# Two-column copies on VectorE, second keys and values ahead of the third query, a tick after every k tile of the even layer

## The chip, the cores and the metric

The kernel runs on one core of one Trainium2 chip. The metric is device time in microseconds (us) of one execution. Engines are named as the profile names them: PE is TensorE (PEld its weight loads), DVE is VectorE, ACT is ScalarE, POOL is GpSimd, SP is the queue that issues nearly all DMAs.

## The reference, cut to what matters

One inference step of a two-layer trunk over 128 context tokens and 512 latent tokens (640 columns, `T`), width 2048, all fp32. Each layer is an adaLN-modulated RMS norm, one wide input projection, two mixers side by side, a SiLU gate, an output projection and a gated residual:

```python
def modulation(cond, w, b):
    m = jax.nn.silu(cond) @ w + b
    return jnp.split(m, 3, axis=-1)          # shift, scale, gate: for layer 0 and layer 1

def even_mixer(h, w_in, sink, wg, bg, gnorm, cache):
    qa, ka, va, qb, kb, vb, rb, gp = split_cols(h @ w_in, EVEN_SPLITS)
    ya = window_sink_attention(rope_2d(qa), rope_2d(ka), va, ck, cv, sink)   # 8 query heads, 2 key-value heads
    yb, s_fin = gla_branch(qb, kb, vb, rb, wg, bg, gnorm, s0)                # 4 heads, two directions
    y = jnp.concatenate([ya, yb.astype(ya.dtype)], axis=-1) * jax.nn.silu(gp)
    return y, side
...
        x = x + gate[:, None] * (y @ w_out[l])
```

The context tokens go through the same weights with plain causal-free attention; the odd layer has neighbourhood attention and a spatial-gating MLP in the two mixers' places.

## The kernel before

**Tiling.** Activations lie feature-major: 16 tiles (`KT`) of 128 features by 2 + 640 columns. The two columns in front carry the shift vectors of the two request groups, so that one matmul chain also gives the projection of the shift. A projection makes one *chunk* of 128 output features at a time: 16 k tiles, two halves of the columns (322 and 320 wide), and three matmuls each, because a fp32 product is made of two reduced-precision parts of each operand: `acth`/`actl` of the activations, `whi`/`wlo` of the weights. That is 96 matmuls of 320 or 322 columns a chunk, called projection matmuls below. A chunk's weights come by DMA into `wraw` (later `rs`), ACT makes `whi`, and POOL (sometimes DVE) subtracts to make `wlo`.

**Evacuation.** When a half of a chunk is complete in its PSUM bank, `evac` in `lin` or `gate` multiplies it by `rstd` on DVE into an SBUF tile; for the first half it also copies the two shift columns to a small tile `bc` (L1378 in `lin`, L1408 in `gate`), which a later ACT instruction adds as a bias. Until the product and the copy are both done the bank isn't free for the next half.

**Stages.** The start (modulation of layer 0, norm, first chunks) takes the first 165 us; then the gated linear attention (GLA) of the even layer, four heads, to about 510 us; then the even attention, eight heads, to about 740 us; then the output projection and the odd layer, most of it as Strassen products of chunk pairs (`spair`), to the end.

**What sets the order.** The program is written by a planner. The class `Pace` keeps a modelled clock for each engine; `Trunk.now` is PE's. The projection matmuls are the backbone. Everything else (heads, GLA steps, splits of weights, deferred halves of evacuations) is a Python generator that is advanced by `tick()`. One tick issues due DMAs, deferred evacuations, up to three weight splits, one task step, and up to four steps of the low-priority task `ada_task`. In `units` (L890 to L909), which runs the plain chunks, a tick comes after every second k tile: that is after six projection matmuls. A step is issued when `until` says that its operands are ready within 0.05 on the modelled clock.

`need(flags)` is the one place where the backbone stops: where the next evacuation needs a buffer that a head still holds, the planner moves its clock and calls `tick` until the flag comes, and no projection matmul is issued meanwhile. The engines run their queues in order, so such a place is a run of head matmuls with nothing between them.

`ada_task` computes the modulations that are needed later (names `partg`, `parts`, `part`, in the order gate 0, scale 1, shift 1, gate 1) on DVE, as reductions of 128x512 (last table 128x256) from `adas` against a row that ACT has put in a PSUM bank. It may step while DVE's modelled clock is no more than `room` ahead of PE's; `rooms` has one value for each stage.

**The even attention** (L2442 on): chunks stand in the order k0 v0 q0 q1 q2 q3 k1 v1 g0 q4 q5 g1 q6 g2 q7, where g is a gate chunk. There are two query buffers (ring `hq`), so the evacuation of query h needs flag `eq{h-2}`: head h-2 has made its last scores. A head (`even_head`, `blocks`) is a chain of five blocks: scores on PE, maximum on DVE, exponential on ACT, normalization on DVE, transposes on PE, copies on DVE and ACT, and at the end one product with the values.

```python
                pre = (f"eq{h - 2}",) if h >= 2 else ()
                add(wE[h], 128, True, None, lazy("hq", SC, pre=pre, then=qdone))
```

## Time and profile before

| | us |
|---|---|
| median of 3 runs (2110.97 to 2112.99) | 2111.03 |
| the profiled execution | 2111.34 |
| its span, first to last instruction | 2109.6 |
| mean granted TensorE clock | 0.995 |

| engine | busy, us | share of the span |
|---|---|---|
| PE | 2054.4 | 97% |
| DVE | 1518.0 | 72% |
| POOL | 1047.1 | 50% |
| ACT | 970.3 | 46% |

PE is what the other engines serve. It was idle for 55 us of the span; a shorter time has to come out of that, out of stretches in which its clock was lowered, or out of fewer matmuls. The table by stages and the waits of PE stand in the prediction.

### The profile page before, as it was taken

How to read it: one execution, taken by the hardware profiler on the slowest of the kernel's cores; microseconds unless marked ns; L12 is line 12 of the kernel's file. 1: busy time of each engine (PE TensorE's matmuls, PEld its weight loads, DVE VectorE, ACT ScalarE, POOL GpSimd, SP SyncE). 2: the span in 40 equal slices, each digit the busy share in tenths (PEclk: the TensorE clock that was granted, in tenths of full speed). 3: DMA queues.
4: the chain of work that ended last, by engine and by line, in shares of the span. 5: the costliest groups of instructions: out<-in, count | busy, mean ns of one | idle time of the engine just before them, and what ended most of it. 6: DMA issues, size and time to landing. Idle time of an engine off the chain costs nothing. (4 is left out here: it accounts for less than half of the span.)

```text
span 2109.6 us, 38920 instructions
## 1 busy us (share of the span) xinstructions
PE 2054.4 (97%) x13990; PEld 1978.4 (94%) x13990; DVE 1518.0 (72%) x3367; ACT 970.3 (46%) x2100; POOL 1047.1 (50%) x797
## 2 busy tenths in 40 slices
PE   7999999999999999999999999999999999999996
PEld 4789999999989999999999999999999999999996
DVE  1337786777887876798766898887787777776565
ACT  3334454353343445544454444444555554454443
POOL 3433343233313223476656565656555557649783
PEclk9999999999999999999999999999999999999998
DMA  9955432335544443677658756656666565568766
GB/s 373 326 190 154 128 109 93 120 125 166 175 122 161 141 148 105 212 255 235 203 138 276 258 202 215 231 192 208 214 214 213 185 234 203 168 209 261 244 199 217
DMA packets 216306, 412.48 MB, mean 196 GB/s; under 512 B 25712, under 2 KB 89008, under 8 KB 216112
## 3 DMA queue, kind: packets, MB, share of 16 engines
q1 hardware_dynamic: 214640, 408.43, 58.9%
q8 instruction: 110, 1.80, 0.3%
q10 hardware_dynamic: 1472, 1.56, 0.2%
q14 instruction: 84, 0.69, 0.1%
HBM read 368.83 MB, written 38.45 MB: 193 GB/s over the span
## 5 line engine op out<-in xcount | busy, mean ns | idle before, releaser
L394 PE MATMUL bank<-acth,whi 128*128 128x320 f32 (+1 forms) x3144 | 963.8, 318 | 12.7 <-DVE arena L208 3.5
L394 PE MATMUL bank<-acth,wlo 128*128 128x320 f32 (+1 forms) x3144 | 939.2, 310 | 5.8 <-POOL wlo L208 5.6
L394 PE MATMUL bank<-actl,whi 128*128 128x320 f32 (+1 forms) x3144 | 937.6, 310 | 0.0
L208 POOL TENSOR_TENSOR wlo<-wraw,whi 128x512 fp32r<-128x512 f32 x351 | 483.1, 1382 | 726.6 <-ACT whi L208 652.7
L394 PEld LDWEIGHTS bank<-acth,whi 128*128 128x128 f32 x3144 | 583.1, 188 | 31.3 <-issue 9.8
L394 PEld LDWEIGHTS bank<-acth,wlo 128*128 128x128 f32 x3144 | 582.7, 188 | 8.7 <-POOL wlo L208 8.7
L394 PEld LDWEIGHTS bank<-actl,whi 128*128 128x128 f32 x3144 | 583.1, 188 | 1.5
L208 POOL TENSOR_TENSOR wlo<-rs,whi 128x512 fp32r<-128x512 f32 x285 | 401.7, 1421 | 217.8 <-ACT whi L208 193.0
L208 ACT ACTIVATE whi<-wraw 128x512 fp32r<-128x512 f32 (+1 forms) x397 | 243.0, 624 | 177.0 <-PE bank L394 105.6
L208 ACT ACTIVATE whi<-rs 128x512 fp32r<-128x512 f32 x329 | 200.4, 624 | 72.1 <-PE bank L394 46.2
L208 DVE CUSTOM_DVE_ANT_0 adas<-adas,bank,partg 128x256 bf16<-128x256 f32 (+1 forms) x320 | 178.1, 556 | 17.1 <-ACT bank L208 6.9
L394 PE MATMUL bank<-tail,whi 128*128 128x322 f32 (+1 forms) x672 | 152.1, 313 | 0.0
L394 PE MATMUL bank<-eh,whi 128*128 128x322 f32 (+1 forms) x444 | 139.2, 314 | 0.0
L394 PE MATMUL bank<-eh,wlo 128*128 128x322 f32 (+1 forms) x444 | 138.0, 311 | 0.0
L394 PE MATMUL bank<-el,whi 128*128 128x322 f32 (+1 forms) x444 | 137.7, 310 | 0.0
L208 ACT ACTIVATE bc<-bank 128x2 f32<-128x2 f32 (+1 forms) x101 | 17.2, 170 | 230.4 <-DVE arena L208 148.1
L208 ACT ACTIVATE Y<-bank 128x128 f32<-128x128 f32 (+5 forms) x134 | 52.0, 411 | 133.1 <-PE bank L394 77.8
L394 PEld LDWEIGHTS bank<-tail,whi 128*128 128x128 f32 x672 | 112.3, 189 | 0.4
L208 DVE TENSOR_TENSOR rs<-rs 128x512 f32<-128x512 f32 x83 | 89.2, 1085 | 26.7 <-POOL wlo L208 26.4
L208 DVE TENSOR_TENSOR bank<-bank,sums 128x320 f32<-128x320 f32 (+1 forms) x162 | 76.4, 492 | 40.8 <-PE bank L394 33.0
L394 PE MATMUL bank<-tail,wlo 128*128 128x322 f32 (+1 forms) x336 | 104.0, 309 | 0.0
L208 ACT ACTIVATE arena<-arena,bc 128x192 f32<-128x192 f32 (+4 forms) x167 | 82.5, 518 | 42.0 <-DVE arena L208 40.2
(215 smaller groups left out, 2901.6 us busy)
## 6 DMA issues: line engine op xcount, KB each, us to landing
tail<-far_dram SPq DMA_DIRECT2D x196, 322.0 KB, 4.2
wraw<-w_even SPq DMA_DIRECT2D x176, 256.0 KB, 3.3
adas<-ada_g SPq DMA_DIRECT2D x128, 256.0 KB, 4.3
adas<-ada SPq DMA_DIRECT2D x128, 256.0 KB, 3.6
rs<-w_odd SPq DMA_DIRECT2D x63, 512.0 KB, 5.1
Y<-ada SPq DMA_DIRECT2D x37, 512.0 KB, 6.0
wraw<-w_odd SPq DMA_DIRECT2D x37, 512.0 KB, 5.3
rs<-w_out SPq DMA_DIRECT2D x30, 512.0 KB, 5.6
```

Source lines behind the costliest of these rows:

```text
L208: return f(*args, **kw)
L394: self.nc.tensor.matmul(out, lhsT, rhs, start=start, stop=stop, **kw)
```

## The change

Four edits. The two-column copies go from ACT to DVE, in `lin` and in `gate`. The chunks of the even attention are made from a list, `ORDER`, in which k1 and v1 stand ahead of q2 and q3; v1 now names its need of `v0`, since both pass through one buffer. `units` ticks after every k tile. `rooms[0]`, which holds until the even attention opens, goes from 0.3 to 0.5.

```diff
+ORDER = "k0 v0 q0 q1 k1 v1 q2 q3 g0 q4 q5 g1 q6 g2 q7".split()
...
-    rooms, calms, lags = (0.3, 1.2, 1.5, 0.8), (4.0, 2.0), (3.0, 3.0, 2.0, 1.0, 0.4)
+    rooms, calms, lags = (0.5, 1.2, 1.5, 0.8), (4.0, 2.0), (3.0, 3.0, 2.0, 1.0, 0.4)
...
                     self.mm_k(c, j, [(p[half], half)], k0)
-                    if j % 2:
+                    if True:
                         self.tick()
...
-                nc.scalar.activation(bc[:M], pa[:M, 0:2], AF.Copy, scale=scale)
+                nc.vector.tensor_scalar(bc[:M], pa[:M, 0:2], scale, None, ALU.mult)
...
-                nc.scalar.activation(bc, pa[:, 0:2], AF.Copy)
+                nc.vector.tensor_copy(bc, pa[:, 0:2])
...
-        for kv in range(2):
...
-            add(wE[8 + kv], 128, True, None, lazy("hk", then=kdone))
-            add(wE[10 + kv], 128, True, None, lazy("av", then=vdone))
-            for h in range(4 * kv, 4 * kv + 4):
-                if kv and h != 5:
-                    i = max(h - 5, 0)
-                    gate_chunk(wE[28 + i], i, (f"ya{i}",), "gx")
...
+            add(wE[10 + kv], 128, True, None, lazy("av", pre=("v0",) if kv else (), then=vdone))
...
+            add(wE[h], 128, True, None, lazy("hq", SC, pre=(f"eq{h - 2}",) if h >= 2 else (), then=qdone))
...
+        for x in ORDER:
+            n = int(x[1])
+            if x[0] == "g":
+                gate_chunk(wE[28 + n], n, (f"ya{n}",), "gx")
+            else:
+                {"k": att_k, "v": att_v, "q": att_q}[x[0]](n)
```

The built programs, instruction by instruction: PE has the same 13,200 instructions in another order (the first 1,170 and the last 2,459 stand in the same order). ACT loses 101 two-column copies and 2 table loads, DVE gains the 101 copies. Since the planner decides by its clocks which engine makes a `wlo`, 20 of them go from DVE to POOL (POOL 632 to 652, DVE 90 to 70).

The first place is on PE, in the even attention, where the second head ends. Its scores, transposes (`ident`) and products (names with `Y` and `arena`, the heads' buffers) stand here; rows with `acth` or `actl` are projection matmuls. Before:

```order
L394 MATMUL bank_67<-acth,wlo 128x322
L394 MATMUL bank_70<-Y,arena_4504 128x128
L399 MATMUL bank_71<-ident,arena_4504 128x128 x4
L394 MATMUL bank_72<-Y,arena_4504 128x128
L394 MATMUL bank_72<-arena_4504 128x128
L394 MATMUL bank_72<-Y,arena_4504 128x128
L394 MATMUL bank_70<-arena_4504 128x128
L394 MATMUL bank_70<-Y,arena_4504 128x256
L399 MATMUL bank_71<-ident,arena_4504 128x128 x4
L399 MATMUL bank_72<-ident,arena_4504 128x128
L399 MATMUL bank_70<-ident,arena_4504 128x128 x3
L394 MATMUL bank_71<-Y,arena_4504 128x128
```

The same head's last transposes on PE in the changed program:

```order
L395 MATMUL bank_67<-acth,wlo 128x320
L400 MATMUL bank_72<-ident,arena_4540 128x128 x4
L395 MATMUL bank_67<-acth,whi 128x320
L395 MATMUL bank_67<-actl,whi 128x320
L395 MATMUL bank_67<-acth,wlo 128x320
L395 MATMUL bank_67<-acth,whi 128x320
L395 MATMUL bank_67<-actl,whi 128x320
L395 MATMUL bank_67<-acth,wlo 128x320
L395 MATMUL bank_67<-acth,whi 128x320
L395 MATMUL bank_67<-actl,whi 128x320
L395 MATMUL bank_67<-acth,wlo 128x320
```

Before, 26 head matmuls follow each other with no projection matmul among them, which is the one such run in the even attention (all others have at most 7). In the changed program no run there is longer than 7, and twelve projection matmuls stand between these transposes and the next three.

The second place is on PE in the GLA, at the end of a head: eight and six products, then twelve that need a state which DVE computes after the six. Before:

```order
L394 MATMUL bank_71<-Y,arena_1682 128x128 x8
L394 MATMUL bank_72<-Y,arena_1682 128x128 x6
L394 MATMUL bank_67<-acth,whi 128x320
L394 MATMUL bank_67<-actl,whi 128x320
L394 MATMUL bank_67<-acth,wlo 128x320
L394 MATMUL bank_67<-acth,whi 128x320
L394 MATMUL bank_67<-actl,whi 128x320
L394 MATMUL bank_67<-acth,wlo 128x320
L394 MATMUL bank_70<-Y,arena_1682 128x128 x12
```

And on PE in the changed program:

```order
L395 MATMUL bank_71<-Y,arena_1680 128x128 x8
L395 MATMUL bank_72<-Y,arena_1680 128x128 x6
L395 MATMUL bank_68<-acth,whi 128x320
L395 MATMUL bank_68<-actl,whi 128x320
L395 MATMUL bank_68<-acth,wlo 128x320
L395 MATMUL bank_70<-Y,arena_1680 128x128 x12
```

Between the six and the twelve stand three projection matmuls instead of six; it is so in all four heads.

The third place is the evacuation of q0 in the even attention. Before, the copy stands on ACT, behind three splits of weights:

```order
L208 ACTIVATE Y<-bank_71 128x128
L208 ACTIVATE whi<-wraw 128x512 x3
L208 ACTIVATE bc_4910<-bank_67 128x2
L208 ACTIVATE arena_4504<-arena_4504,bc_4910 128x128
L208 ACTIVATE arena_4504<-arena_4504,bc_4910 128x512
```

In the changed program it stands on DVE, right behind the product from the same bank (the ISA rows are the reductions of `ada_task`):

```order
L209 ISA parts_103 128x1
L209 TENSOR_TENSOR arena_4540<-bank_69,rstd 128x320
L209 TENSOR_SCALAR bc_4947<-bank_69 128x2
L209 ISA adas,parts_103<-adas,bank_73,parts_103 128x512
L209 ISA parts_103 128x1
```

Nothing but the product now stands between the bank's last matmul and its copy on the same engine. The reductions of `ada_task` also stand earlier. Counted on DVE by the number of projection matmuls ahead of them: of gate 1's 128x256 reductions, 14 stand between the 6,900th and the 7,200th before and 26 now, 18 and 29 in the next 300, and 64 and 0 between the 8,400th and the 9,300th.

## Prediction

> **What bounds the kernel now.** I read the engines' busy time first, then the table by stages, then what PE waited for, then the timeline at the largest holes.

> ```profile
> PE 2054.4 (97%) x13990; PEld 1978.4 (94%) x13990; DVE 1518.0 (72%) x3367; ACT 970.3 (46%) x2100; POOL 1047.1 (50%) x797
> ```

> PE works 97% of the span, and the change takes no matmul away. So all that can be won is idle time of PE (2109.6 - 2054.4 = 55.2 us) and time at a lowered clock. The table by stages (columns: PE, PEld, DVE, ACT, POOL busy, granted clock, DMA share, GB/s) says where these lie:

> ```profile
> 0.00:50.00 50.00, 35.96 (x280) 23.94 (x280) 7.47 (x22) 19.22 (x45) 17.07 (x20) 0.97 0.98 371
> ...
> 150.00:500.00 350.00, 346.29 (x2377) 340.87 (x2377) 254.15 (x478) 161.88 (x318) 109.68 (x79) 1.00 0.37 117
> ...
> 520.00:530.00 10.00, 8.04 (x54) 7.50 (x54) 7.94 (x23) 4.29 (x9) 2.77 (x3) 1.00 0.71 247
> 530.00:590.00 60.00, 60.00 (x406) 58.57 (x405) 48.47 (x138) 22.83 (x56) 19.26 (x15) 1.00 0.54 169
> 590.00:604.00 14.00, 9.62 (x50) 7.46 (x49) 12.67 (x46) 4.51 (x17) 0.75 (x1) 0.76 0.24 76
> 604.00:830.00 226.00, 225.85 (x1495) 217.07 (x1494) 168.31 (x492) 99.75 (x237) 62.41 (x49) 1.00 0.45 142
> 830.00:1180.00 350.00, 345.12 (x2333) 343.23 (x2332) 270.49 (x628) 174.78 (x366) 207.71 (x170) 1.00 0.69 218
> 1180.00:1400.00 220.00, 216.67 (x1472) 212.79 (x1471) 188.56 (x381) 97.84 (x215) 132.37 (x93) 1.00 0.64 215
> 1400.00:2000.00 600.00, 595.64 (x3972) 581.18 (x3972) 439.94 (x920) 298.65 (x663) 378.27 (x282) 1.00 0.64 213
> 2000.00:2109.60 109.60, 91.25 (x605) 88.86 (x603) 65.98 (x100) 42.41 (x81) 65.12 (x53) 0.95 0.63 210
> ```

> Start and end hold 14.0 and 18.4 us of the idle time, and PE's order there is untouched. The odd layer and the output projections (830 to 2000) hold 4.9 + 3.3 + 4.4 = 12.6 us, spread thin. The even layer holds 3.7 us in the GLA, 2.0 us at 520 to 530, and 4.4 us at 590 to 604, the only stretch between start and end in which the clock fell (0.76). In the rest of the attention PE is idle for 0.15 us in 286. The whole of PE's waits, largest groups (us, times, longest):

> ```profile
> PE bank L394 <- POOL wlo L208: 5.6, 8, 1.2
> PE bank L394 <- DVE arena L208: 4.9, 8, 1.3
> PE bank L394 <- ACT bc L208: 3.4, 5, 1.2
> ...
> PE bank L394 <- DVE tail L208: 3.2, 2, 1.9
> ...
> PE bank L399 <- DVE arena L208: 2.7, 2, 1.4
> PE bank L399 <- ACT es L208: 1.7, 1, 1.7
> ```

> The last two rows are the hole at 594: 2.7 + 1.7 = 4.4 us.

> **The new order of keys and values.** The timeline of that hole, PE's rows with the idle time before each in brackets:

> ```profile
> 595.65 0.63 PE L399 MATMUL bank<-ident,arena 128*128 128x128 f32 x4 [1.69 <-ACT es L208]
> ...
> 597.54 0.47 PE L399 MATMUL bank<-ident,arena 128*128 128x128 f32 x1 [1.26 <-DVE arena L208]
> ...
> 599.44 0.90 PE L399 MATMUL bank<-ident,arena 128*128 128x128 f32 x3 [1.43 <-DVE arena L208]
> ```

> These are the transposes of the second head, and they are the run of 26 head matmuls of the order before: q3 was due for evacuation, its buffer was q1's, and `need("eq1")` stopped the projections until head 1 had gone through DVE and ACT block by block. With k1 and v1 ahead, q2 and q3 come two chunks later, head 1 ends between projection matmuls, and the run is gone. What is saved is the idle time, 1.69 + 1.26 + 1.43 = **4.4 us**; the 26 matmuls themselves stay. The clock fell in the same place:

> ```profile
> 596.60:600.00 3.40, 1.03 (x4) 0.74 (x5) 3.23 (x15) 1.61 (x7) 0.00 (x0) 0.50 0.01 3
> 600.00:603.40 3.40, 3.40 (x10) 2.34 (x9) 2.60 (x11) 0.28 (x1) 0.00 (x0) 0.50 0.26 77
> ```

> For 6.8 us it was half. PE worked for 1.03 + 3.40 = 4.43 us of that, and at full clock would have needed half: **2.2 us** saved. Waits of up to 1.9 us elsewhere (row DVE tail above, in a stage with a clock of 1.00) did not lower it, so it needs a hole like this one.

> [...]

> What is late next? Behind this wait the next of its kind is q6 on head 4. In the changed order head 4's last scores stand 72 projection matmuls ahead of that evacuation. One takes 60.00 / 406 = 0.148 us (row 530 to 590), so that is 10.6 us of cover. The moved chunks issue the same DMAs of weights and the same four of each rope, at a DMA share of 0.54 and 0.45; I cost that at nothing.

> **The copies.** Rows of the groups by shape (count, busy us, mean ns):

> ```profile
> L208 ACT ACTIVATE bc<-bank 128x2 f32<-128x2 f32 x100 | 17.0, 170 | 229.7 <-DVE arena L208 147.4 <-DVE Y L208 76.7 <-PE bank L394 4.0
> ...
> L208 DVE TENSOR_SCALAR sh<-bank,small 128x2 f32<-128x2 f32 x16 | 3.3, 209 | 0.0
> ...
> L208 DVE TENSOR_TENSOR part_b<-part_b,bank 128x2 f32<-128x2 f32 x15 | 2.2, 149 | 0.0
> ```

> The copy itself isn't in the trace of before on DVE; its bounds are 0.15 and 0.21 us, from DVE's own two-column reads of a bank. I take 0.18: 101 x 0.18 = 18 us of DVE over the whole span, beside PE, while DVE idles 28%. ACT loses 17 us and its order behind DVE. On PE's path it counts where PE waits for the bank, five times:

> ```profile
> 524.59 0.48 DVE L208 TENSOR_TENSOR arena<-bank,rstd 128x320 f32<-128x320 f32 x1
> ...
> 525.11 0.17 ACT L208 ACTIVATE bc<-bank 128x2 f32<-128x2 f32 x1 [4.04 <-DVE arena L208]
> 525.31 0.40 ACT L208 ACTIVATE arena<-arena,bc 128x128 f32<-128x128 f32 x1
> 525.33 0.41 PE L394 MATMUL bank<-acth,whi 128*128 128x320 f32 x1 [0.93 <-ACT bc L208]
> ```

> The copy ended 0.21 us after the product. On DVE it would end 0.15 to 0.21 us after it at the latest. So the engine of the copy is worth 0.1 us a wait at most: 4 x 0.1 = **0.4 us** (0 to 0.5). The wait is long for another reason: DVE began the product late, behind reductions that waited 2.3 us for their DMA while the attention's tables were being loaded (DMA share 0.71).

> That hole, 2.0 us at 520 to 530, has neither its loads nor `room` in that stage changed; but the reductions stand up to some 200 projection matmuls earlier, so their DMAs meet others. I keep half: **1.0 us** saved (0 to 2.0).

> **Finer ticks.** Three projection matmuls instead of six cover DVE's step at the end of each GLA head. What such a step takes is seen uncovered one step earlier:

> ```profile
> 255.26 1.95 PE L394 MATMUL bank<-Y,arena 128*128 128x128 f32 x16
> ...
> 257.02 0.48 DVE L208 SCALAR_TENSOR_TENSOR arena<-arena,etot,bank 128x256 f32<-128x256 f32 x1 [2.17 <-PE bank L394]
> ...
> 257.55 1.60 PE L394 MATMUL bank<-Y,arena 128*128 128x128 f32 x12 [0.35 <-DVE arena L208]
> ```

> By these rows DVE's step of 0.48 us leaves 0.35 us idle when nothing covers it. Three matmuls cover 3 x 0.148 = 0.44 us and hide it, unless DVE is inside a reduction (0.75 us at 128x512), when up to 0.48 + 0.75 - 0.44 = 0.8 us shows: 0 to 3.2 us for four heads. I take **0.3 us** lost. `rooms[0]` at 0.5 lets 0.2 us more of reductions stand ahead of an evacuation in this stage; the second half of a chunk covers that.

> **The stages behind.** PE's work is the same, DVE's is redistributed. From 1246 to 1346 us (the 6,900th to the 7,500th projection matmul) DVE takes 26 + 29 reductions instead of 14 + 18:

> ```profile
> 1246.00:1346.00 100.00, 99.66 (x685) 99.08 (x684) 87.12 (x160) 42.73 (x92) 62.12 (x45) 1.00 0.63 209
> ...
> L208 DVE CUSTOM_DVE_ANT_0 adas<-adas,bank,partg 128x256 bf16<-128x256 f32 x224 | 106.7, 476 | 9.8 <-ACT bank L208 4.3 <-DMA adas<-ada_g 1.1
> ...
> L208 DVE TENSOR_TENSOR wlo<-rs,whi 128x512 fp32r<-128x512 f32 x44 | 52.6, 1199 | 24.9 <-ACT whi L208 24.7
> ```

> That is 23 x 0.476 + 7 copies x 0.18 - 4 splits x 1.2 (gone to POOL) = 10.9 + 1.3 - 4.8 = 7.4 us more, on 87.1 of 100. It still fits, with less slack; relief comes after 1480 us, where PE has no wait to lose. I take **0.5 us** lost over 830 to 2000 (2 us won, as part of the 12.6 goes by another order, to 3 lost).

> **Sum.** -4.4 - 2.2 - 0.4 - 1.0 + 0.3 + 0.5 = -7.2 us on the profiled execution's 2111.3 (span 2109.6): 2104.1. That execution stands 0.3 us above the median of 2111.03, so 2104 either way.

> **Rivals.** *Given back in small waits.* With a tick after three matmuls, a step is issued on average 0.22 us earlier (half of three matmuls), so with that much less between DVE's end and PE's start. The attention has some 88 such handovers (8 heads x 11), the GLA some 40. If two in five came 0.13 us late, 128 x 0.4 x 0.13 = 6.6 us are lost again: 2110.7, no change. Against it: 0.15 us idle in 286 us of attention at the old spacing; a planner that was often late would show it there.

> *The stop moves.* If head 4 runs late by more than its 10.6 us of cover, q6 makes the same hole: 4.4 + 2.2 given back, about 2110.7. Against it: DVE is busy 168 of 226 us in that stretch, with room to catch up.

> *DVE becomes the bound in the odd layer* (the slower side). It decides if less than 7.4 of DVE's 12.9 idle us between 1246 and 1346 can be used. POOL then has four more splits there, and vector additions stand behind these:

> ```profile
> L208 POOL TENSOR_TENSOR wlo<-rs,whi 128x512 fp32r<-128x512 f32 x285 | 401.7, 1421 | 217.8 <-ACT whi L208 193.0 <-PE bank L394 8.1 <-DVE partg L208 4.9
> ...
> L208 DVE TENSOR_TENSOR rs<-rs 128x512 f32<-128x512 f32 x83 | 89.2, 1085 | 26.7 <-POOL wlo L208 26.4
> ```

> With none usable, 7.4 + 4 x 1.42 = 13.1 us lie on PE's path: 2104.1 - 0.5 + 13.1 = 2116.7, slower. [...] Against it: with 87% busy, PE lost only 0.3 us there.

> **How the numbers follow.** Chances: the forecast 0.74, small waits 0.12, the stop moved 0.07, DVE the bound 0.07. The forecast's own range: at best -4.4 - 2.2 - 0.5 - 2.0 - 2 = -11.1 (2100), at worst -4.4 - 2.2 + 1.5 + 3 = -2.1 (2109). Both rivals of no change lie at 2110.7, so the range goes to 2111; what is left out is the slower rival and the tails. 0.2% of 2111, about what a measurement of this kernel tells from no change, is 4.2 us, so faster means below 2106.8: most of the forecast, 0.71. The same: its upper part and the two rivals, 0.23. Slower: 0.06.

> **What would show it.** Right: no row of PE waiting for `es` or for transposed blocks near 590 to 610, clock 1.00 from 50 to 2090; 3 us or less idle from 150 to 500 beyond today's 3.7 would bound the ticks' cost; DVE above 93% from 1246 to 1346 with PE's idle time there below 2 us. Wrong: a new clock dip, PE waits in many groups below 0.5 us in the attention, or over 16 us idle from 830 to 2000.

## The result, and the profile after

| | median, us | runs |
|---|---|---|
| before | 2111.99 | 4 (2110.97 to 2112.99) |
| changed | 2100.79 | 4 (2099.39 to 2104.05) |
| ratio | 0.995 | 95% interval 0.9935 to 0.9965 |

The change wins 11.2 us, a little over 0.5%; the forecast was about 7. The profiled execution took 2099.8 us, its span is 2098.0 us. The engines' busy time, on the page of the changed kernel:

```profile
PE 2050.6 (98%) x13990; PEld 1977.5 (94%) x13990; DVE 1500.2 (72%) x3448; ACT 962.7 (46%) x1997; POOL 1080.6 (52%) x817
```

PE's idle time went from 55.2 to 47.4 us. The table by stages of the changed kernel (columns as before: PE, PEld, DVE, ACT, POOL busy, granted clock, DMA share, GB/s):

```profile
150.00:500.00 350.00, 347.55 (x2390) 342.45 (x2389) 274.45 (x557) 160.03 (x295) 119.36 (x81) 1.00 0.40 128
...
520.00:530.00 10.00, 9.21 (x65) 8.93 (x64) 7.45 (x22) 3.85 (x8) 3.04 (x3) 1.00 0.69 220
530.00:590.00 60.00, 58.53 (x394) 56.34 (x393) 51.42 (x147) 24.08 (x61) 17.34 (x13) 1.00 0.51 155
590.00:604.00 14.00, 14.00 (x89) 12.87 (x88) 12.77 (x37) 4.72 (x10) 3.04 (x3) 1.00 0.54 171
604.00:830.00 226.00, 225.31 (x1497) 216.86 (x1496) 175.36 (x512) 100.42 (x228) 63.06 (x49) 1.00 0.46 142
830.00:1180.00 350.00, 346.12 (x2343) 344.23 (x2342) 270.27 (x661) 174.92 (x363) 209.43 (x171) 1.00 0.69 219
1180.00:1400.00 220.00, 218.66 (x1490) 215.53 (x1490) 187.03 (x461) 100.55 (x209) 145.61 (x103) 1.00 0.68 229
1400.00:2000.00 600.00, 596.54 (x3986) 583.51 (x3986) 403.49 (x805) 294.70 (x617) 398.89 (x296) 1.00 0.61 204
```

Two things are to be seen. The hole is gone: from 590 to 604 PE is busy all the time at full clock, where it had 9.62 of 14 at 0.76. And from 830 to 2000, where the prediction expected a small loss, the idle time fell from 12.6 to 3.88 + 1.34 + 3.46 = 8.7 us. What PE waited for in the changed kernel (us, times, longest):

```profile
PE bank L395 <- DVE arena L209: 4.4, 8, 1.2
...
PE bank L395 <- POOL wlo L209: 2.4, 3, 1.2
PE bank L400 <- DVE arena L209: 2.1, 2, 1.4
...
PE bank L395 <- DVE bc L209: 1.3, 2, 1.0
```

The wait for POOL's `wlo` was 5.6 us in 8 places and is 2.4 in 3. That row points at the part of the gain that the prediction didn't see.

Since windows of time shift between kernels, the kernels are compared below by marks in PE's own work: the time between its 640th, 4,400th and 11,800th projection matmul, read from the trace of each kernel's profiled execution (counted by all PE matmuls that are 320 or 322 columns wide). "Even" is GLA and even attention, "odd" the output projections and the odd layer. The start and the last 55 to 59 us are left out, since they vary by up to 3 us between executions of one kernel. One execution of e9, the profiled one (10650 us), and one of the kernel before beside e5 to e8 (5869 us) were disturbed and are left out of every median and ratio, so e9 has no row here. Each cell is us, and behind it idle PE / time at half clock:

| kernel | even | odd |
|---|---|---|
| before | 695.9, 10.7 / 6.8 | 1190.7, 10.9 / 0 |
| changed | 688.3, 5.8 / 0 | 1185.2, 7.5 / 0 |
| copies alone, plan kept (e1) | 693.7, 9.6 / 3.4 | 1184.9, 5.9 / 3.4 |
| copies alone, planned anew (e2) | 690.1, 7.0 / 3.4 | 1187.6, 9.0 / 3.4 |
| order alone (e3) | 686.9, 5.1 / 0 | 1200.4, 14.9 / 10.2 |
| ticks alone (e4) | 691.4, 8.5 / 0 | 1208.3, 21.0 / 10.2 |
| changed, copies back on ACT (e6) | 691.1, 8.1 / 0 | 1210.9, 21.2 / 20.5 |
| copies and order (e7) | 686.2, 4.6 / 0 | 1190.9, 10.5 / 6.8 |
| copies, ticks, rooms (e8) | 689.1, 7.1 / 0 | 1181.3, 5.4 / 0 |

So the change won 7.6 us in the even layer, as forecast, and 5.4 us in the odd layer, where of the four edits only the copies act directly.

### The profile page after: what moved, and what is told of

Its sections match the earlier page's. It is cut to its first block, busy times and chain, and to the rows that moved or that the text cites. A ratio compares the mean times of both kernels' runs of the same rounds, so it can differ in the third digit from the quotient of the medians.

```text
span 2098.0 us, 39027 instructions
## 1 busy us (share of the span) xinstructions
PE 2050.6 (98%) x13990; PEld 1977.5 (94%) x13990; DVE 1500.2 (72%) x3448; ACT 962.7 (46%) x1997; POOL 1080.6 (52%) x817
## 5 line engine op out<-in xcount | busy, mean ns | idle before, releaser
L209 POOL TENSOR_TENSOR wlo<-wraw,whi 128x512 fp32r<-128x512 f32 x364 | 507.1, 1399 | 705.7 <-ACT whi L209 609.1
L209 POOL TENSOR_TENSOR wlo<-rs,whi 128x512 fp32r<-128x512 f32 x292 | 411.6, 1423 | 192.6 <-ACT whi L209 179.3
L209 ACT ACTIVATE whi<-rs 128x512 fp32r<-128x512 f32 x329 | 201.3, 625 | 110.1 <-PE bank L395 55.2
L209 DVE TENSOR_TENSOR bank<-bank,sums 128x320 f32<-128x320 f32 (+1 forms) x162 | 76.7, 494 | 61.1 <-PE bank L395 49.8
L209 ACT ACTIVATE sums<-bank 128x320 f32<-128x320 f32 (+1 forms) x125 | 54.4, 436 | 107.9 <-PE bank L395 104.8
```

The lines of the kernel that those rows point to most:

```text
L209: return f(*args, **kw)
```

## The experiments

Medians are quoted beside the kernel before, run with them on the same chip: 2112.12 us (23 runs) for e1 to e4, 2111.5 (10) for e5 to e8, 2112.28 (11) for e9 to e12. Ratios are of means.

### The copies by themselves (e1, e2)

e1 is the kernel before with both copies on DVE, but entered into the planner's clocks as ACT's. So nothing is planned anew: every engine's order stays, and only the copies change engine.

```diff
-                nc.scalar.activation(bc[:M], pa[:M, 0:2], AF.Copy, scale=scale)
+                self.pace.record("a", "activation", (bc[:M], pa[:M, 0:2]), {})
+                self.tc.nc.vector.tensor_scalar(bc[:M], pa[:M, 0:2], scale, None, ALU.mult)
```

and the same with a copy in `gate`. e2 has the two lines of the change's own diff, so the planner knows, and plans anew.

> The 101 two-column copies run on DVE, but the planner goes on as if ACT ran them, so PE, POOL, SP and all other instructions of ACT and DVE stand in the order of before. Theory A (a copy on ACT waits for DVE's product and holds the weight splits queued behind it): PE's waits for wlo between 1200 and 1850 us, 3.9 us in the profile of before, go, and the time falls by 3 to 4.5 us, to 2107.5 to 2109. Theory B (what was won behind 830 us came from the other plan: splits moved to POOL, reductions moved forward): within 1 us of before, 2111 to 2113, with the waits for wlo still there.

> Only the copies go to DVE, and the planner knows it. Theory A: the same 3 to 4.5 us as with the plan kept, 2107.5 to 2109; the hole at 594 us with its half clock stays. Theory B: 3 to 5 us here and nothing with the plan kept.

Measured: e1 2106.14 us (12 runs), ratio 0.9967 [0.9956, 0.9977]; e2 2106.04 us (5 runs), 0.9967 [0.9954, 0.998]. The copies win 6.0 us, more than was expected, and planning anew adds nothing: Theory A holds with a larger size, and Theory B falls. The same place of the odd layer shows how. The timeline of ACT and POOL in the kernel before, two of PE's waits behind it, and DVE's product that they trace back to (start, us; idle time before in brackets):

```profile
1197.20 0.62 ACT L208 ACTIVATE whi<-rs 128x512 fp32r<-128x512 f32 x1
...
1203.00 0.49 DVE L208 TENSOR_TENSOR Y<-bank,rstd 128x320 f32<-128x320 f32 x1
...
1203.53 0.17 ACT L208 ACTIVATE bc<-bank 128x2 f32<-128x2 f32 x1 [5.71 <-DVE Y L208]
1203.59 1.14 ACT L208 ACTIVATE whi<-rs 128x512 fp32r<-128x512 f32 x2
...
1204.27 0.41 PE L394 MATMUL bank<-acth,whi 128*128 128x320 f32 x1 [0.32 <-ACT whi L208]
1204.30 1.27 POOL L208 TENSOR_TENSOR wlo<-rs,whi 128x512 fp32r<-128x512 f32 x1 [5.10 <-ACT whi L208]
...
1205.62 0.42 PE L394 MATMUL bank<-acth,wlo 128*128 128x320 f32 x1 [0.79 <-POOL wlo L208]
```

ACT stood idle for 5.71 us in front of a copy of 0.17 us, because DVE was late with its product from the same bank: the copy began 0.04 us after the product's end. Behind the copy stood two splits of weights that need neither. ACT kept to the order of its queue for those 5.71 us, and the splits began 0.06 us after the copy began. POOL had waited 5.10 us for them, and PE then waited for ACT's part of the weights (0.32 us) and for POOL's (0.79 us). The same instructions in e1, in the same order but for the copy:

```profile
1196.06 1.93 ACT L208 ACTIVATE whi<-rs 128x512 fp32r<-128x512 f32 x3
1196.77 3.00 POOL L208 TENSOR_TENSOR wlo<-rs,whi 128x512 fp32r<-128x512 f32 x2 [1.71 <-ACT whi L208]
...
1202.28 0.15 DVE L1379 TENSOR_SCALAR bc<-bank 128x2 f32<-128x2 f32 x1
...
1202.80 0.44 ACT L208 ACTIVATE sums<-bank 128x320 f32<-128x320 f32 x1 [4.82 <-PE bank L394]
```

All three splits are done by 1197.99, over 4 us before the copy, and PE has no wait of 0.3 us here. DVE is as late as it was (its product begins 6.14 us after ACT's last `sums` in both); its lateness no longer reaches PE. All of e1's waits for `wlo` together fell from 5.6 us in 8 places to 2.6 in 3.

A rival is that e1 wins by freeing the banks earlier. The traces speak against it. In the odd layer (862 to 2045 us), where e1 wins 5.8 us by the marks, PE waits for the copy itself in one place, 0.29 us before and 0.25 in e1. The wait for `wlo` goes from 3.3 us in 6 places to 0.3 in 1 there, and for `whi` from 0.8 in 2 to none.

### The order and the ticks by themselves (e3, e4)

e3 has the list `ORDER` of the change, e4 `if True:` for `if j % 2:` in `units`; all else is the kernel before.

> Only k1 and v1 go ahead of q2 and q3. Theory A: the run of 26 head matmuls goes, 4.4 us of idle time and 2.2 us of half clock with it: 6.6 us, 2105 to 2106, and the clock is 1.00 from 50 to 2090 us. Rival: head 1 is still late for something, and a hole of over 2 us comes back within 60 us: 2108 to 2112.

> Only the tick after every k tile. Theory A: the stop for head 1 stays, since the order of the chunks makes it; the four GLA waits grow from 0.35 us by at most 0.1 each: 2111 to 2113. Rival: heads get through faster with more ticks, so that the stop shrinks: 2107 to 2110. Second rival: small waits in many groups, over 2 us together: 2114 or more.

Measured: e3 2112.07 us (12 runs), ratio 0.9997 [0.9988, 1.0007]; e4 2122.4 us (6 runs), 1.0046 [1.003, 1.0062]. The order does what it says in its own place. From a table by windows of e3, the attention and a stretch of the odd layer:

```profile
525.00:845.00 320.00, 318.96 (x2127) 308.51 (x2127) 243.44 (x676) 143.35 (x340) 93.73 (x71) 1.00 0.43 135
...
1180.00:1400.00 220.00, 215.13 (x1441) 210.34 (x1440) 189.84 (x404) 96.60 (x214) 137.90 (x96) 0.99 0.64 215
```

PE is idle for 1.0 us in 320, and by the marks the even layer is 9.0 us shorter. But the odd layer is 9.7 us longer, and the total stands still, so that the 2105 to 2106 of Theory A fail. The finer ticks alone win 4.5 us in the even layer (the run of 26 head matmuls is gone there too; the longest has at most 8) and lose 17.6 in the odd one. Of the times expected for e4 only the second rival's, 2114 or more, holds. PE's waits in e3, whole groups:

```profile
PE bank L395 <- POOL wlo L209: 6.5, 9, 1.2
...
PE bank L395 <- DVE tail L209: 4.5, 2, 4.1
PE bank L395 <- ACT whi L209: 3.5, 4, 1.6
```

The longest, 4.1 us for `tail`, stands at the start of the odd layer, and the clock falls behind it (granted 0.99 from 845 to 1180 us; pairs of matmuls take 0.74 us from 1068.26 us on, and 0.46 before the wait); waits for `tail` stay in e7 below, where the copies are on DVE (4.6 us in 2). The other two rows fall to 2.2 us in 2 and 1.1 in 1 there, and what they are the timeline of e3 shows at one place:

```profile
1310.33 0.48 DVE L209 CUSTOM_DVE_ANT_0 adas<-adas,bank,partg 128x256 bf16<-128x256 f32 x1
...
1311.26 0.56 DVE L209 TENSOR_TENSOR arena<-bank,rstd 128x128 f32<-128x128 f32 x2
...
1311.85 0.17 ACT L209 ACTIVATE bc<-bank 128x2 f32<-128x2 f32 x1 [6.52 <-DVE arena L209]
1311.92 0.62 ACT L209 ACTIVATE whi<-rs 128x512 fp32r<-128x512 f32 x1
...
1312.60 0.42 PE L395 MATMUL bank<-acth,whi 128*128 128x320 f32 x1 [1.29 <-ACT whi L209]
1313.94 0.64 PE L395 MATMUL bank<-acth,wlo 128*128 128x320 f32 x1 [0.79 <-POOL wlo L209]
```

It is the same chain: reductions of `ada_task` stand in front of DVE's product, ACT waits 6.52 us at its copy, and the splits behind the copy come late, here by 1.29 + 0.79 us of PE's time, and one period of half clock follows (window of e3):

```profile
1313.75:1317.16 3.41, 3.21 (x12) 3.22 (x13) 2.96 (x6) 1.84 (x5) 3.35 (x3) 0.50 0.47 138
```

So what the prediction counted on for the order is won in the even layer and lost again in the odd one. Both edits let `ada_task` run differently. Counted by projection matmuls ahead of it, the first of gate 1's 224 reductions stands behind some 5,480 in the kernel before, 6,280 in e3 and 5,420 in e4, and the last behind some 9,150, 9,310 and 8,820. That the moved reductions are what makes DVE late is argued from this: no run holds them in place while order or ticks change.

### The parts together (e5 to e8)

The theory after e1 to e4 (C in the expectations): order and ticks move the reductions into busy places of the odd layer, the lateness of DVE reaches PE through ACT's copy, and so their gain lasts only with the copies on DVE. The rival (D): the parts add up, each with its own price. e5 is the changed kernel again; e6 the changed kernel, its plan kept, with both copies issued on ACT; e7 has copies and order, no finer ticks, `rooms[0]` at 0.3; e8 is the changed kernel with the old order of the chunks.

```diff
 e6
-                nc.vector.tensor_scalar(bc[:M], pa[:M, 0:2], scale, None, ALU.mult)
+                self.pace.record("v", "tensor_scalar", (bc[:M], pa[:M, 0:2]), {})
+                self.tc.nc.scalar.activation(bc[:M], pa[:M, 0:2], AF.Copy, scale=scale)
 e7
-    rooms, calms, lags = (0.5, 1.2, 1.5, 0.8), (4.0, 2.0), (3.0, 3.0, 2.0, 1.0, 0.4)
+    rooms, calms, lags = (0.3, 1.2, 1.5, 0.8), (4.0, 2.0), (3.0, 3.0, 2.0, 1.0, 0.4)
...
-                    if True:
+                    if j % 2:
 e8
-ORDER = "k0 v0 q0 q1 k1 v1 q2 q3 g0 q4 q5 g1 q6 g2 q7".split()
+ORDER = "k0 v0 q0 q1 q2 q3 k1 v1 g0 q4 q5 g1 q6 g2 q7".split()
```

> The changed kernel as it is, on one chip with the next three. Both theories: 0.993 to 0.9965 of before, about 2101 where before takes 2112.

> The changed kernel with its copies on ACT again, while the planner goes on as if DVE ran them: PE, POOL, SP and everything else stand in the order of the changed kernel. Theory C (late products on DVE cost PE little as long as the weight splits on ACT do not stand behind the copy; order and ticks move reductions into the odd layer's busy places, so that their gain lasts only with the copies on DVE): more is lost than the 6 us that the copies alone were worth, 2110 or more, with waits for wlo back between 1150 and 1800 us. Theory D (the parts add up): 6 us lost, 2106 to 2108.

> Copies on DVE and the new order, ticks and rooms as before. Theory C: 6.0 from the copies and the 6.6 of the stop now last: 2098.5 to 2101.5. Theory D: 6 from the copies and nothing from the order: 2105 to 2107.

> The changed kernel with the old order of the chunks. With ticks after every k tile the planner no longer stops for head 1 (its longest run of head matmuls is 7 here too), so by theory C order and ticks are two remedies for one stop: within 1.5 us of the changed kernel, no hole of over 2 us and no lowered clock in the attention. Theory D: ticks alone lost 10 us, so without the order's help 2111 or more. Rival of both: the order is needed beside the ticks, 2104 to 2108, with a hole near 595 us.

| | median, us | ratio, 95% |
|---|---|---|
| e5 changed | 2103.17 | 0.9958 [0.9945, 0.9972] |
| e6 copies back | 2123.04 | 1.005 [1.0036, 1.0065] |
| e7 copies and order | 2100.04 | 0.9945 [0.9931, 0.9958] |
| e8 old order | 2096.29 | 0.9932 [0.9919, 0.9945] |

e6 settles by which way the loss reaches PE. It differs from e5 in the engine of 101 tiny copies alone, and is 19.9 us slower; in the plan of before the same move was worth 6.0. The parts don't add: alone, copies, order and ticks would give -6.0 + 0 + 10.3, about +4 in all (`rooms[0]` wasn't tried alone), and the whole gives -8.3 beside these runs. The same place of the odd layer on ACT, and on PE behind it; first e6:

```profile
1443.29 0.44 ACT L209 ACTIVATE sums<-bank 128x322 f32<-128x322 f32 x1 [3.02 <-PE bank L395]
...
1447.83 0.17 ACT L1380 ACTIVATE bc<-bank 128x2 f32<-128x2 f32 x1 [2.02 <-DVE arena L209]
1447.92 0.63 ACT L209 ACTIVATE whi<-rs 128x512 fp32r<-128x512 f32 x1
...
1454.40 0.77 PE L400 MATMUL bank<-ident,Y 128*128 128x128 f32 x5 [2.19 <-ACT Y L209]
```

Then the changed kernel:

```profile
1429.86 0.44 ACT L209 ACTIVATE sums<-bank 128x322 f32<-128x322 f32 x1 [3.02 <-PE bank L395]
...
1431.50 0.63 ACT L209 ACTIVATE whi<-rs 128x512 fp32r<-128x512 f32 x1
...
1439.29 0.77 PE L400 MATMUL bank<-ident,Y 128*128 128x128 f32 x5 [0.51 <-ACT Y L209]
```

From `sums` to the split of `rs` it is 1.64 us, and with the copy in between 4.63. PE's wait at the head that follows is 0.51 and 2.19 us. The steps between can be followed in both traces, counted from the start of `sums`: POOL's `wlo` from `rs` begins 3.67 us after it in the changed kernel and 5.34 in e6, and DVE's next addition to `rs`, which waits for that `wlo`, 4.99 and 6.66. Both are late by 1.67 us in e6, and PE's wait is longer by 1.68. In the odd layer PE waits for the copy itself 0.3 us in one place in either kernel, so freeing the bank is no rival here. The price is larger than in the plan of before because the clock falls too: by the marks e6's odd layer has 13.7 us more idle time and 20.5 us at half clock, which is an estimated 10 us (half of it, on busy PE).

One caution: e6's planner believes the copies on DVE, so it puts splits behind them more freely than it would otherwise. But e3 and e4, whose planner knew of copies on ACT, lose 12.0 us against e7 and 17.3 against e9 below, across chips, and there too the copies are the only edit that differs.

e7 lies where Theory C put it, some 5 us below Theory D's range. e8 was not foreseen to be the fastest, and misses Theory C's time, within 1.5 us of the changed kernel, by some 5 us: the run of 26 head matmuls is gone without the new order too (its longest run in the attention is 7). Order and ticks are two remedies for one stop.

### What the new order is worth beside the ticks (e9 to e12)

e9 is e8 with `rooms[0]` at 0.3, e10 the changed kernel with `rooms[0]` at 0.3, e11 e8 again, e12 the changed kernel a third time.

> Copies on VectorE and finer ticks, the old order of the chunks, rooms[0] at 0.3. Three theories of what the new order is worth beside the finer ticks. Theory E (the order costs by itself beside the ticks, since the stop at head 1 is already gone with them and k1, v1 ahead of q2, q3 only moves reductions of gate 1 back into busier places): this kernel stands with copies, ticks and rooms at 0.5 (2096.3 so far), within 4 us, and both stand 4 us or more below the two kernels that have the new order. Theory F (rooms at 0.5 made the difference): this kernel falls back to 2101 or more, and only the kernel with rooms at 0.5 and the old order stands near 2096. Theory G (chance: the 7 us came from where the periods of half clock fell in that call): all four kernels of this call lie within 4 us of each other.

> The changed kernel with rooms[0] back at 0.3 and nothing else undone. Theory E: 2100 to 2104, as the changed kernel, 4 us or more above copies and ticks. Theory F (rooms): with the new order too rooms at 0.3 is worse, 2105 or more. Theory G (chance): within 4 us of all others of this call.

> The changed kernel with the old order of the chunks, a second time on another call. Theory E and Theory F: again 2094 to 2099, 4 us or more below the changed kernel beside it. Theory G (chance): up to 2100 to 2104, no different from the changed kernel.

> The changed kernel unchanged, as the standard of this call: 2100 to 2104 by all theories.

| copies and ticks, with | `rooms[0]` 0.3 | `rooms[0]` 0.5 |
|---|---|---|
| old order | e9 2105.1, 0.9965 [0.9952, 0.9977] | e11 2098.93, 0.993 [0.9919, 0.9942] |
| new order | e10 2103.22, 0.9956 [0.9944, 0.9968] | e12 2101.84, 0.9952 [0.9939, 0.9966] |

Theory E falls, since e9 isn't within 4 us of e11. Theory G falls, since those two are 6.2 us apart with intervals that don't meet. Theory F holds for the old order alone: with the new one `rooms[0]` makes 1.4 us, within the runs' spread. So no price or worth of the new order by itself is shown: it goes with 2 us less at one setting and 3 us more at the other, and at each the two intervals overlap. e8 and e11 are one kernel, 10 runs with a median of 2097.6 us, against 2102.0 for the 12 runs of e5 and e12, each on two chips: the change without its new order is faster than the change by about 4 us, and the fastest version found. e7, copies and order alone, has 2100.0 from 5 runs on one chip, and its interval meets those of both. What makes these last few us isn't settled: by the marks, e8 and e11 gain on the changed kernel in the odd layer (1181.3 us in both, against 1185.2 to 1187.0), spread over several places.

## Why the prediction was right, and where it wasn't

**The hole (-4.4 and -2.2): right.** The three waits are gone, the clock is 1.00, and in e3, with nothing else changed, the time from the 2,600th to the 4,300th projection matmul falls from 328.0 to 319.2 us. That is 8.8, about the 6.6 of the hole and the 2.0 at 520 to 530 together. But e4 and e8 show that the finer ticks remove the run as well, which the prediction gave to the order alone.

**The copies (-0.4): the term that was mis-sized.** They measure -6.0. The step that failed is "So the engine of the copy is worth 0.1 us a wait at most". It priced the copy only where PE waits for the bank, and looked at what is ahead of it. As a price of those waits it was near: in e1 four of the five changed by -0.14, +0.02, -0.19 and -0.04 us; the fifth, 0.93, is gone, and PE's next wait is 0.20 longer. It didn't ask what is queued behind it: splits of weights on ACT, then POOL, then PE's `wlo`, a row of 5.6 us, the largest wait that the prediction quoted, and given to no term. The size of one copy was right: 0.15 us on DVE in the rows above, forecast 0.18.

**The stages behind (+0.5): the stage moved the other way.** By the marks it gives -5.4. e1, the copies alone, gives -5.8 there, so beside the copies the moved work costs 0.4 us, or 1.0 and 2.1 by the profiles of e5 and e12. The term itself was of the right size there, and the gain is the copies'. With the old order (e8, e11) the same stage gives -9.4. The fear behind the term was sound: order and ticks alone cost 9.7 and 17.6 us there. It was not DVE's capacity, though: the copy on ACT carried DVE's lateness on to the splits, and the change removes that carrier. So the rival of DVE as the bound falls in the place that it named:

```profile
1236.00:1336.00 100.00, 100.00 (x689) 99.86 (x689) 86.59 (x209) 43.85 (x84) 67.02 (x48) 1.00 0.68 229
```

DVE is at 86.6%, not above 93, and PE never idles.

**520 to 530 (-1.0) and the ticks in the GLA (+0.3): right to a us.** The idle time went from 1.96 to 0.79 us. The gap of 0.35 us stands once in each GLA head, as before, and three matmuls cover the next step.

**Small waits, and the stop moved to q6: not seen.** From 604 to 830 PE idles 0.69 us. One wait is new and was not foreseen, and it eats part of the even layer's gain (timeline of the changed kernel):

```profile
551.31 1.27 POOL L209 TENSOR_TENSOR wlo<-wraw,whi 128x512 fp32r<-128x512 f32 x1 [4.51 <-PE bank L395]
...
551.36 1.23 DVE L209 TENSOR_TENSOR den<-den,es 128x1 f32<-128x1 f32 x1
...
553.17 0.33 PE L400 MATMUL bank<-ident,arena 128*128 128x128 f32 x1 [1.44 <-DVE arena L209]
```

One column takes DVE 1.23 us (the mean of the 40 like it is 0.29), until 0.01 us after POOL's split ends; the head behind it is late by 1.44 us.

The forecast of 2104 and its range to 2100 thus held, with one large cause left out. The even layer's terms sum to -7.3 and measured -7.6; the odd layer's, with the copies, to about 0 and measured -5.4. The even layer's sum is so close in part by luck: PE's waits for the copy at 203.78 and 495.81 us (0.79 and 0.19) went too, and two new waits (1.44, and 0.69 at 627.25) took 2.1 us back. That the total lies inside the range, 0.8 us above its lower end, is luck too: that end had 2 us for the stages behind and 2 for 520 to 530, and nothing for the splits behind the copy.

## What to carry to other kernels

Price an instruction by what stands behind it in its engine's queue, not only by who waits for its result: here a copy of 0.17 us that waited 5.71 us for DVE held the splits queued after it that long, and the engine of such copies was worth 6 us in one plan and 20 in another. Put such an instruction on the engine whose result it waits for anyway. In a kernel that a planner lays out, test edits together and apart: two remedies for one stop don't add, and an edit can lose alone what it wins beside another.

## What the runs showed of the hardware that was not expected

The prediction said that waits of up to 1.9 us don't lower the clock. They did in some runs. In e1 a wait of 1.79 us for `tail` is followed by 3.41 us at half clock:

```profile
1072.72 1.00 PE L394 MATMUL bank<-acth,whi 128*128 128x322 f32 x2 [1.79 <-DVE tail L208]
```

```profile
1068.80:1073.04 4.24, 2.44 (x16) 2.04 (x14) 4.23 (x8) 1.74 (x4) 0.23 (x1) 1.00 0.23 72
1073.04:1076.45 3.41, 3.41 (x13) 3.37 (x13) 0.23 (x1) 2.15 (x5) 1.74 (x2) 0.50 0.75 274
```

In the changed kernel the wait at the same matmul is longer, and the clock stays:

```profile
1070.72 0.78 PE L395 MATMUL bank<-acth,whi 128*128 128x322 f32 x2 [1.92 <-DVE tail L209]
```

```profile
1070.70:1076.00 5.30, 5.28 (x32) 4.93 (x33) 0.33 (x1) 4.25 (x9) 4.12 (x5) 1.00 0.16 62
```

Most of these periods between start and end last 3.41 us (as in e1 here and in e3 at 1313.75 us), the others 6.83 (as in the kernel before at 596.62 us). The changed kernel went either way: its first two profiles have no such period here, and its third, e12, has one after a wait of 1.99 us:

```profile
1066.48 0.78 PE L395 MATMUL bank<-acth,whi 128*128 128x322 f32 x2 [1.99 <-DVE tail L209]
```

```profile
1067.38:1070.79 3.41, 3.41 (x15) 3.41 (x14) 0.79 (x2) 2.11 (x4) 1.28 (x2) 0.50 0.79 288
```

At the granted 0.50 each such period on busy PE costs an estimated 3.41 / 2 = 1.7 us, which goes some way to explain why one kernel's runs spread over 10 us: in e12 the fastest, 2098.2 us, has a granted clock of 0.996 and the slowest, 2108.6, of 0.993, and 0.003 of the time is about 6 us.
